# Block 2's mixing weights split into two parts during block 1's w_down and kept in DRAM; memory keys and values made earlier; the HGRN tail by head pair

## The chip, the cores and the metric

The kernel runs on one core of one Trainium2 chip. Its time is in device microseconds (us) from the start to the end of the program on that core. Engines are named as in the profile: PE is the matrix engine, PEld its weight loads, DVE the vector engine, ACT the activation engine, POOL GpSimd, SP the engine that issues most DMAs (its queue is SPq; ACTq is ACT's own).

## The reference, cut to what matters

Two transformer blocks run on 512 positions of width 1024 in float32. Block 1 mixes (convolution, block-sparse attention, memory attention, gates) and ends with a feed-forward net, FFN1: `w_up`, a convolution, gelu, `w_down`. Block 2, whose weights have the suffix `_2`, is what the change is about:

```python
h = rmsnorm_2(x, norm_mix[layer])
hq, hf, hi, hg, sq, sk, sv, iq, ik, iw, mq = split_in(h @ w_in[layer])
o_hg = hgrn2_mix(hq, hf, hi, hg, lb[layer], out_gain[layer])   # gated linear recurrence
o_sa = dsa_mix(sq, sk, sv, iq, ik, iw, ...)                    # top-256 keys by an index score
mem_n = rmsnorm_2(mem, norm_mem[layer])
o_mem = mem_mix(mq, mem_n, w_mem_kv[layer], ...)               # keys and values from mem alone
mixed = jnp.concatenate([o_hg, o_sa, o_mem], axis=-1)
x = x + mixed @ w_out[layer]
h = rmsnorm_2(x, norm_ffn[layer])
a, b = jnp.split(h @ w_ffn_in[layer], 2, axis=-1)
x = x + (silu(a) * b) @ w_ffn_out[layer]
```

The memory keys and values of block 2 need `mem_2` and `w_mem_kv_2` alone, and the split of a weight needs the weight alone; neither needs an activation.

## The kernel before, in words

**Products in three passes.** Every large product is made in the float32r type: each operand is split into a rounded part hi and a remainder lo, and PE does hi·hi, hi·lo and lo·hi (L175 to L177). Weights come in tiles of 128x1024 float32 (512 KB). `load` (L187) has SP bring a raw tile into one of three buffers of `rawp`; `split` has ACT make hi (a cast, L197) and then DVE make lo (a subtraction, L198). With `pr.on_pool` POOL does the subtraction; that is set for 16 tiles of block 2's mixing, w_mqsv to w_hq (the second half). hi and lo of a streamed tile take two of six buffers of `wp`, so three tiles are ready at most; "hold" and "res" tiles take buffers of the general pool `sp` (38 of 128x1024).

**Order of the work.** `Program` (L44 to L165) is a list of jobs, each with its weight tiles, written down in program order; each engine then runs its own instructions in that order. Before a job is recorded, tiles are loaded and split for it and up to two streamed tiles beyond (four "hold", six "res"). Background generators (index scores, top-k rounds, the recurrence, the attentions) advance by one step at each tick, a tick being one job or one part of a job, times their rate; `drain` runs a generator to its end. An engine stops where its next instruction has to wait, and what stands behind it in its order waits too.

**Stages of the time before.** QKV, convolution, attention and gates to 441 us; w_out to 487; `w_up` of FFN1 to 733; `w_down` to 855 (22 tiles of 24 matmuls; the last 4 are taken for each quarter of the positions in turn). Then block 2's mixing: w_hf and w_hq (first halves), w_ikw, w_iq, w_mqsv, w_mkv2, w_sqk, w_hf and w_hq (second halves), w_hi, w_hg. In the background run the gates, `hgrn_levels` (rate 0.5; DVE L1274 belongs to it), `idx` (index scores, then `top_keys`: rounds of MAX8, L1007, and MATCH_REPLACE8, L1008), the build of `memT2` (norm and transposes of the memory), the memory attention `mem2` and the selected attention `sa0` and `sa1`, one for each pair of heads. After w_hg `hgrn_levels` is drained, and `hgrn_tail` makes the output of the recurrence for all four heads of one quarter of the positions at a time: products L1399, square on ACT (L1401), sum on DVE, a power on POOL, scaling on DVE (L1406), the gate on POOL (L1408), transposes and L270/L275. w_out_2 follows in four steps of K (kp 0 to 3); kp 0 needs `mem2`, kp 1 needs `sa0` and `sa1`, kp 2 and 3 need the tail. L601 is the normalising of attention weights on ACT, L307 a transpose on PE, L618 attention weights times values. The second feed-forward net runs from 1200 us to the end.

## Time and profile before

| what | value |
|---|---|
| median of 3 runs | 1567.25 us (1565.92 to 1567.9) |
| the profiled execution's own time | 1568.02 us |
| its span, first to last instruction | 1566.2 us |
| mean granted clock of TensorE | 0.986 |
| chain that ended last, by engine | PE 82%, DVE 7%, ACT 4%, POOL 2%, issue 2%, DMA 2% |
| HBM read and written | 145.66 MB and 4.85 MB |

The span lies 1.8 us inside the execution's own time. Busy time of an engine is a share of the span; the chain says which engine's work ended last at each step. Times in us from the start of the span place a stage.

### The profile page before, as it was taken

To read this page: it belongs to the slowest core of one execution; us is meant where nothing else is said; L and a number is where in the kernel's file an instruction comes from. 1 tells how busy PE (TensorE), PEld (TensorE's weight loads), DVE (VectorE), ACT (ScalarE), POOL (GpSimd) and SP (SyncE) were. 2 spreads that over 40 slices of the span, in tenths; PEclk is the share of its full clock that TensorE was granted. 3 is DMA by queue.
4 is the path that set the end of the run, shared out by engine and by line. 5 is a ranking of instruction groups with operands and counts; after the bars stand their busy time and mean duration, and the time that the engine had idled before them with its cause. 6 is when DMAs were issued, how large, how long until landed. Compare 5 with 4: busy or idle time off the path is not lost.

```text
span 1566.2 us, 20399 instructions
## 1 busy us (share of the span) xinstructions
PE 1520.0 (97%) x8107; PEld 1261.1 (81%) x8107; DVE 789.3 (50%) x1200; ACT 597.5 (38%) x1043; POOL 238.3 (15%) x344
## 2 busy tenths in 40 slices
PE   8999999999999999999999999999789999999999
PEld 7887888888888888888888977677568888888887
DVE  5455453544446666665235488988545233333231
ACT  5454452433343433333234465455533222222120
POOL 1000000021102000000002197716220000000000
PEclk9999999999999999999999999999699999999999
DMA  5432243322252122223232331122222122222231
GB/s 187 99 106 73 83 128 108 121 81 81 96 164 78 68 95 99 102 96 107 95 137 92 115 119 70 68 75 82 68 81 81 68 94 95 94 102 100 94 121 54
DMA packets 46053, 151.83 MB, mean 97 GB/s; under 512 B 5476, under 2 KB 5988, under 8 KB 45958
## 3 DMA queue, kind: packets, MB, share of 16 engines
q1 hardware_dynamic: 41472, 142.62, 26.6%
q10 hardware_dynamic: 4486, 7.90, 1.8%
q8 instruction: 64, 1.05, 0.3%
q14 instruction: 31, 0.25, 0.0%
HBM read 145.66 MB, written 4.85 MB: 96 GB/s over the span
## 4 chain that ended last, share of the span: by engine, by line
PE 82%; DVE 7%; ACT 4%; POOL 2%; issue 2%; DMA 2%; ACTq 0%; SPq 0%; DVEq 0%; POOLq 0%
PE p L175 26%; PE p L176 26%; PE p L177 26%; PE p L307 2%; ACT s L592 1%; DVE s L1008 1%; DVE s L1274 1%; DVE m L1007 1%; PE p L618 1%; ACT s L601 1%; POOL m L228 1%; DVE wl L198 1%; DMA s<-mem 0%; POOL s L183 0%; DVE s L180 0%
## 5 line engine op out<-in xcount | busy, mean ns | idle before, releaser
L175 PE MATMUL p<-s,wh 128*128 128x512 f32 (+1 forms) x1192 | 463.6, 389 | 0.9 <-DVE t L1314 0.6
L176 PE MATMUL p<-s,wh 128*128 128x512 f32 (+1 forms) x1192 | 461.0, 387 | 0.0
L177 PE MATMUL p<-s,wl 128*128 128x512 f32 (+1 forms) x1192 | 460.7, 387 | 0.0
L198 DVE TENSOR_TENSOR wl<-r,wh 128x1024 fp32r<-128x1024 f32 x217 | 258.3, 1192 | 329.8 <-ACT wh L197 329.0
L197 ACT CAST wh<-r 128x1024 fp32r<-128x1024 f32 x233 | 232.9, 1002 | 230.8 <-PE p L176 219.2
L175 PEld LDWEIGHTS p<-s,wh 128*128 128x128 f32 x1192 | 224.0, 188 | 46.3 <-DVE t L1314 0.8
L177 PEld LDWEIGHTS p<-s,wl 128*128 128x128 f32 x1192 | 223.9, 188 | 45.5
L176 PEld LDWEIGHTS p<-s,wh 128*128 128x128 f32 x1192 | 224.0, 188 | 43.9
L175 PE MATMUL p<-wh,s 128*128 128x512 f32 x544 | 218.6, 402 | 4.1 <-ACT s L270 4.1
L177 PE MATMUL p<-wh,s 128*128 128x512 f32 x544 | 215.2, 396 | 1.0 <-DVE s L275 0.5
L176 PE MATMUL p<-wl,s 128*128 128x512 f32 x544 | 214.8, 395 | 0.0
L176 PE MATMUL p<-s,s 128*128 128x256 f32 (+1 forms) x408 | 132.2, 324 | 5.6 <-DVE s L180 5.6
L175 PE MATMUL p<-s,s 128*128 128x256 f32 (+1 forms) x408 | 133.2, 326 | 0.9 <-ACT s L268 0.8
L177 PE MATMUL p<-s,s 128*128 128x256 f32 (+1 forms) x408 | 131.6, 322 | 0.0
L183 POOL TENSOR_SCALAR s<-t 128x512 fp32r<-128x512 f32 (+1 forms) x64 | 34.7, 543 | 618.3 <-DVE t L1506 227.4
L175 PEld LDWEIGHTS p<-wh,s 128*128 128x128 f32 x544 | 104.0, 191 | 26.3 <-ACT s L270 4.5
L177 PEld LDWEIGHTS p<-wh,s 128*128 128x128 f32 x544 | 103.8, 191 | 24.2 <-DVE s L275 1.0
L176 PEld LDWEIGHTS p<-wl,s 128*128 128x128 f32 x544 | 104.1, 191 | 20.5
L176 PEld LDWEIGHTS p<-s,s 128*128 128x128 f32 x408 | 79.5, 195 | 11.9 <-DVE s L180 6.6
L175 PEld LDWEIGHTS p<-s,s 128*128 128x128 f32 x408 | 79.4, 195 | 7.1 <-ACT s L268 1.5
L177 PEld LDWEIGHTS p<-s,s 128*128 128x128 f32 x408 | 79.5, 195 | 5.3
L307 PE MATMUL p<-ident,s 128*128 128x128 f32 x400 | 59.7, 290 | 16.2 <-ACT s L601 4.8
(182 smaller groups left out, 1416.1 us busy)
## 6 DMA issues: line engine op xcount, KB each, us to landing
r<-w_up SPq DMA_DIRECT2D x44, 512.0 KB, 3.2
r<-w_ffn_in SPq DMA_DIRECT2D x44, 512.0 KB, 3.2
r<-w_in_gate SPq DMA_DIRECT2D x24, 512.0 KB, 3.2
r<-w_down SPq DMA_DIRECT2D x22, 512.0 KB, 3.2
r<-w_ffn_out SPq DMA_DIRECT2D x22, 512.0 KB, 3.2
r<-w_out SPq DMA_DIRECT2D x16, 512.0 KB, 3.2
r<-w_in_conv SPq DMA_DIRECT2D x12, 512.0 KB, 3.2
r<-w_in_qk SPq DMA_DIRECT2D x8, 512.0 KB, 4.6
```

What stands on the lines that cost most here:

```text
L175: mm(out, sh, mh, start=start, stop=False)
L176: mm(out, sh, ml, start=False, stop=False)
L177: mm(out, sl, mh, start=False, stop=stop)
L183: g_.tensor_scalar(out, x, s, 0.0, op0=ALU.mult, op1=ALU.add)
L197: a_.copy(hi[:, :n], raw)
L198: (g_ if on_pool else v_).tensor_tensor(out=lo[:, :n], in0=raw, in1=hi[:, :n].bitcast(F32), op=ALU.subtract)
L228: g_.tensor_tensor(out=rs, in0=ms, in1=negh[:, :n], op=ALU.pow)
L307: pe.transpose(ps[:m, n:n + P], s, ident)
L592: a_.activation(pv, pv, AF.Exp, scale=-1.0, bias=negm[s][:, i:i + 1], accum_out=sums[s][:, i:i + 1])
L601: a_.activation(pv, pv, AF.Copy, scale=rec[s][:, i:i + 1])
L618: mm(ps[64 * s:64 * s + 64, j * P:512], vh(s, j), p_view(PT, s, 3 - j), start=(j == 0), stop=(j == 3))
L1007: v_.max(m8, sc)
```

## The change

1. `pr.on_pool` goes; wherever a split is still made in place, DVE makes lo (now L204; the cast is L203, the raw load L189).
2. `Parts`: the 29 tiles of block 2's mixing weights (w_hf 4, w_hq 4, w_ikw 1, w_iq 4, w_mqsv 4, w_sqk 4, w_hi 4, w_hg 4) are split by a generator, "splits", at rate 0.5 during w_down. For each tile SP loads the raw tile into a buffer of `sp` (L216), ACT casts (L218), DVE subtracts (L219), and SP stores hi (L221) and lo (L222) to a DRAM tile `wd`. In the mixing, `split` loads both parts by two DMAs (L199, L200) into the buffers that the products read.
3. `memT2` is built from job 3 of w_up on, and the products with w_mkv2 and the finish of the keys (`fin_mkv2`) follow in w_up.
4. The mixing's products come in the order w_hf, w_hq (first halves), w_ikw, w_iq, w_mqsv, w_hf, w_hq (second halves), w_sqk, w_hi, w_hg. w_hg is now made in the transposed form, by chunks, and its weight is packed for that.
5. The tail is made per pair of heads j and half of the positions; `tail0` runs during w_hg. The gate's product is one DVE instruction with the gain (L1467) in place of a POOL one, then a cast on ACT (L1472) and a subtraction on DVE. `sa` runs the two pairs of the selected attention one after the other. w_out_2's kp 0 needs `mem2`, kp 1 `sa`, kp 2 and 3 `tail0` and `tail1`.

```diff
     def load(src):
+        if isinstance(src, Parts):
+            return src
         raw = rawp.tile([P, 1024], F32, tag="raw", name=nm("r"))[:, :src.shape[-1]]
         nc.sync.dma_start(raw, src)
         return raw
 
-    def split(raw, resident, on_pool):
-        n = raw.shape[-1]
+    def split(raw, resident):
         if resident:
             hi, lo = slot([P, 1024], F32R), slot([P, 1024], F32R)
         else:
             hi = wp.tile([P, 1024], F32R, tag="w", name=nm("wh"))
             lo = wp.tile([P, 1024], F32R, tag="w", name=nm("wl"))
+        if isinstance(raw, Parts):
+            nc.sync.dma_start(hi.bitcast(F32), raw.d[0])
+            nc.sync.dma_start(lo.bitcast(F32), raw.d[1])
+            return hi, lo
+        n = raw.shape[-1]
         a_.copy(hi[:, :n], raw)
-        (g_ if on_pool else v_).tensor_tensor(out=lo[:, :n], in0=raw, in1=hi[:, :n].bitcast(F32), op=ALU.subtract)
+        v_.tensor_tensor(out=lo[:, :n], in0=raw, in1=hi[:, :n].bitcast(F32), op=ALU.subtract)
         return hi, lo
+
+    class Parts:
+
+
+        def __init__(self, src):
+            self.src = src
+
+        def make(self):
+            raw, hi, lo = slot([P, 1024]), slot([P, 1024], F32R), slot([P, 1024], F32R)
+            self.d = drp.tile([2, P, 1024], F32, name=nm("wd"))
+            nc.sync.dma_start(raw, self.src)
+            yield
+            a_.copy(hi, raw)
+            v_.tensor_tensor(out=lo, in0=raw, in1=hi.bitcast(F32), op=ALU.subtract)
+            yield
+            nc.sync.dma_start(self.d[0], hi.bitcast(F32))
+            nc.sync.dma_start(self.d[1], lo.bitcast(F32))
 
     pr = Program(load, split)
...
     for j in range(2, NFF):
+        if j == 3:
+            pr.start("memT2", lambda: memT2.build())
+        if j == 8:
+            pr.drain("memT2")
+            gemm_N([io["w_mkv2"][i] for i in range(4)], lambda: memT2, lambda t, ps: use_mkv2(t, ps), nt=2)
+            pr.start("kv2", lambda: fin_mkv2())
         chunk(W[j], H, use_up_a(j))
         chunk(W[NFF + j], H, use_up_g(j))
-
+    pr.drain("kv2")
+
+    M = {n: [Parts(io[n][j]) for j in range(io[n].shape[0])]
+         for n in ("w_hf", "w_hq", "w_iq", "w_mqsv", "w_sqk", "w_hi", "w_hg")}
+    M["w_ikw"] = [Parts(io["w_ikw"])]
+    order = [M[n][c] for n in ("w_hf", "w_hq") for c in (0, 1)] + M["w_ikw"] + M["w_iq"] + M["w_mqsv"]
+    order += [M[n][c] for n in ("w_hf", "w_hq") for c in (2, 3)] + M["w_sqk"] + M["w_hi"] + M["w_hg"]
+
+    def splits():
+        made = [p.make() for p in order]
+        for n in range(len(made) + 2):
+            for p in made[max(0, n - 2):n + 1]:
+                next(p, None)
+            yield
+
+    pr.start("splits", splits, 0.5)
...
-    def hgrn_out(t):
+    def hgrn_out(j, tp):
+
         ps = bank()
-        for hd in range(4):
-            j, i2 = hd // 2, hd % 2
-            o = ps[:, hd * P:(hd + 1) * P]
-            ops = []
-            if t >= 2:
-                for s in range(2):
-                    ops.append((hg["o256"][j][:, i2, s, (t - 2) * P:(t - 1) * P], s))
-            if t % 2 == 1:
-                ops.append((hg["o128"][:, hd, t // 2, :], t - 1))
-            ops.append((hg["ATd"][j][:, i2, t, :], t))
-            for n, (l, s) in enumerate(ops):
-                mm(o, l, hi_[s // 2][:, s % 2, hd * P:(hd + 1) * P], start=(n == 0), stop=(n == len(ops) - 1))
+        for tt in range(2):
+            t = 2 * tp + tt
+            for i2 in range(2):
+                hd = 2 * j + i2
...
                          in1=rs[:, :, None].to_broadcast([P, 4, P]), op=ALU.mult)
-        g_.tensor_tensor(out=y, in0=y, in1=gS[t // 2][:, t % 2, :], op=ALU.mult)
         return y
...
+    def hgrn_outT(j, tp, y):
+
+        pt = transposes([y[:, (2 * t + k) * P:(2 * t + k + 1) * P] for k in range(2) for t in range(2)])
+        cols = slice(tp * 256, tp * 256 + 256)
+        z = tmp()
+        v_.scalar_tensor_tensor(z.rearrange("p (k t) -> p k t", k=2), pt.rearrange("p (k t) -> p k t", k=2),
+                                vcol(V_HG), gS[j][:, :, cols], op0=ALU.mult, op1=ALU.mult)
+        mixed.alloc(j)
+        hi, lo = mixed.h[j][:, :, cols], mixed.l[j][:, :, cols]
+        z = z.rearrange("p (k t) -> p k t", k=2)
+        a_.copy(hi, z)
+        sub_lo(lo, z, hi)
+
+    def hgrn_tail(j):
+        def g():
+            while ("done", 2 * j + 1) not in hg:
+                yield
+            y1 = hgrn_out(j, 1)
+            yield from wait(2)
+            y0 = hgrn_out(j, 0)
+            yield from wait(2)
+            while ("gate", j) not in hg:
+                yield
+            hgrn_outT(j, 1, y1)
+            yield from wait(2)
+            hgrn_outT(j, 0, y0)
+        return g
...
     def mixing():
-        next_head((late2, swap2), [io[n][c] for n in ("w_hf", "w_hq") for c in (0, 1)],
+        next_head((late2, swap2), [M[n][c] for n in ("w_hf", "w_hq") for c in (0, 1)],
                   [use_hf(0), use_hf(1), use_hq(0), use_hq(1)], park)
         pr.start("gates0", gates(0))
         pr.start("hgrn", hgrn_levels, 0.5)
-        chunk(io["w_ikw"], H, use_ikw)
+        chunk(M["w_ikw"][0], H, use_ikw)
         pr.start("idx", chain(sel0, index_weights, *(index_scores(c) for c in range(4)), top_keys(3),
                               top_keys(2), top_keys(1)), 0.6)
         for c in range(4):
-            chunk(io["w_iq"][c], H, use_iq(c))
-        pr.on_pool = True
-        pr.start("memT2", memT2.build)
-        gemm_N([io["w_mqsv"][j] for j in range(4)], H, use_mqsv)
+            chunk(M["w_iq"][c], H, use_iq(c))
+        gemm_N(M["w_mqsv"], H, use_mqsv)
         pr.start("finm", fin_mq)
-        pr.drain("memT2")
-        gemm_N([io["w_mkv2"][j] for j in range(4)], lambda: memT2, use_mkv2, nt=2)
-        pr.start("mem2", chain(fin_mkv2, mem2_pair(0), mem2_pair(1)), 0.5)
-        gemm_N([io["w_sqk"][j] for j in range(4)], H, use_sqk)
+        for c in (2, 3):
+            chunk(M["w_hf"][c], H, use_hf(c))
+        pr.drain("finm")
+        pr.start("mem2", chain(mem2_pair(0), mem2_pair(1)), 0.5)
+        for c in (2, 3):
+            chunk(M["w_hq"][c], H, use_hq(c))
+        pr.start("gates1", gates(1))
+        gemm_N(M["w_sqk"], H, use_sqk)
         pr.start("fin", fin_sqk)
-        for c in (2, 3):
-            chunk(io["w_hf"][c], H, use_hf(c))
-        for c in (2, 3):
-            chunk(io["w_hq"][c], H, use_hq(c))
-        pr.start("gates1", gates(1))
-        pr.rate("idx", 0.6)
-        pr.start("sa0", sa_pair(0), 0.5)
-        pr.start("sa1", sa_pair(1), 0.5)
-        pr.on_pool = False
-        gemm_N([io["w_hi"][j] for j in range(4)], H, use_hi)
-        gemm_N([io["w_hg"][j] for j in range(4)], H, use_hg)
-        pr.drain("hgrn")
-        pr.start("tail", hgrn_tail, 1.0)
+        gemm_N(M["w_hi"], H, use_hi)
+        pr.start("tail0", hgrn_tail(0))
+        pr.start("sa", chain(sa_pair(0), sa_pair(1)), 0.5)
+        pr.start("tail1", hgrn_tail(1))
+        for c in range(4):
+            chunk(M["w_hg"][c], H, use_hg(c))
...
-             need={0: ("mem2",), 1: ("sa0", "sa1"), 2: ("tail",)})
+             need={0: ("mem2",), 1: ("sa",), 2: ("tail0", "tail1")})
```

**SP in w_down.** Before, SP's order there held loads of w_down alone:

```order
L187 DMA r_6037<-w_down 128x1024
L187 DMA r_6067<-w_down 128x1024
L187 DMA r_6097<-w_down 128x1024
L187 DMA r_6127<-w_down 128x1024
L187 DMA r_6157<-w_down 128x1024
```

In the changed program one tile of w_down (r, from w_down) comes with two raw tiles of the mixing (s, from w_ikw and w_iq) and the stores of two others (wd):

```order
L189 DMA r_6157<-w_down 128x1024
L221 DMA wd_6130<-s_6128 128x1024
L222 DMA wd_6130<-s_6129 128x1024
L216 DMA s_6175<-w_ikw 128x1024
L221 DMA wd_6151<-s_6149 128x1024
L222 DMA wd_6151<-s_6150 128x1024
L216 DMA s_6196<-w_iq 128x1024
L189 DMA r_6205<-w_down 128x1024
```

Between two loads of w_down there now stand six more DMAs of 512 KB; a raw load stands behind the stores of an earlier tile.

**ACT in w_down.** Before, its casts there are those of w_down tiles (wh from r):

```order
L197 CAST wh_6033<-r_5947 128x1024
L197 CAST wh_6063<-r_5977 128x1024
L197 CAST wh_6093<-r_6007 128x1024
L197 CAST wh_6123<-r_6037 128x1024
L197 CAST wh_6153<-r_6067 128x1024
```

In the changed program two casts of mixing tiles (s from s) stand between two of w_down:

```order
L203 CAST wh_6201<-r_6063 128x1024
L218 CAST s_6197<-s_6196 128x1024
L218 CAST s_6224<-s_6223 128x1024
L203 CAST wh_6249<-r_6109 128x1024
L218 CAST s_6245<-s_6244 128x1024
L218 CAST s_6272<-s_6271 128x1024
L203 CAST wh_6297<-r_6157 128x1024
```

The cast of a w_down tile (wh_6297, whose raw load r_6157 is the first row of SP's piece above) now stands behind casts of mixing tiles whose raw loads SP issues later than r_6157: s_6271 is two loads of w_down later.

**PE at kp 1 of w_out_2.** Before, the products with the values (L618) of both pairs (p_9732, p_9745) stand side by side there, and each pair's scores long before:

```order
L1399 MATMUL p_9714<-s_8872,s_7002 128x128 x2
L1399 MATMUL p_9714<-s_8872,s_7003 128x128 x2
L618 MATMUL p_9732<-s_9516,s_7571 64x512 x2
L618 MATMUL p_9732<-s_9523,s_7571 64x384 x2
L618 MATMUL p_9732<-s_9528,s_7571 64x256 x2
L618 MATMUL p_9732<-s_9523,s_7571 64x128 x2
L618 MATMUL p_9745<-s_9535,s_7571 64x512 x2
L618 MATMUL p_9745<-s_9542,s_7571 64x384 x2
L618 MATMUL p_9745<-s_9547,s_7571 64x256 x2
L618 MATMUL p_9745<-s_9542,s_7571 64x128 x2
L307 MATMUL p_9756<-ident,s_9664 128x128 x4
L175 MATMUL p_9563<-wh_9129,s_9741 128x512
```

In the changed program pair 1's scores (L581, L582) stand behind pair 0's products with the values (L641):

```order
L641 MATMUL p_9864<-s_9834,s_7912 64x512 x2
L641 MATMUL p_9864<-s_9841,s_7912 64x384 x2
L641 MATMUL p_9864<-s_9846,s_7912 64x256 x2
L641 MATMUL p_9864<-s_9841,s_7912 64x128 x2
L581 MATMUL p_9883<-s_8840,s_8837 128x512
L582 MATMUL p_9883<-s_8842,s_8837 128x512
L581 MATMUL p_9886<-s_8840,s_8838 128x512
L582 MATMUL p_9886<-s_8842,s_8838 128x512
```

Pair 1's other twelve score products, its transposes and its own eight products with the values follow with nothing else between, and only then the first pass of kp 1. All of pair 1, from scores to values, now stands behind pair 0.

## Rows read from the trace of the kernel before

**Rows 1.** The page's head, whole program: span, then busy time, share and instructions by engine
```profile
span 1566.2 us, 20399 instructions
...
PE 1520.0 (97%) x8107; PEld 1261.1 (81%) x8107; DVE 789.3 (50%) x1200; ACT 597.5 (38%) x1043; POOL 238.3 (15%) x344
```

**Rows 2.** Windows by stage: bounds, length, busy by engine, granted clock, DMA share, GB/s
```profile
487.00:733.00 246.00, 243.78 (x1166) 206.24 (x1167) 151.11 (x189) 92.90 (x125) 16.11 (x28) 0.99 0.25 88
733.00:855.00 122.00, 122.00 (x548) 101.13 (x546) 45.01 (x50) 36.35 (x59) 7.08 (x13) 1.00 0.34 117
855.00:911.00 56.00, 54.17 (x342) 48.84 (x341) 30.95 (x43) 29.29 (x47) 16.55 (x26) 1.00 0.25 90
911.00:1069.00 158.00, 145.69 (x1064) 111.86 (x1062) 133.80 (x251) 87.52 (x186) 99.85 (x124) 0.98 0.24 82
...
1097.00:1162.00 65.00, 48.24 (x555) 39.20 (x553) 37.14 (x97) 32.77 (x72) 20.95 (x36) 0.79 0.22 72
```

**Rows 3.** Lines in 733:855: count, busy, mean ns, idle before and its releaser
```profile
L177 PE MATMUL p<-wh,s 128*128 128x512 f32 x144 | 56.0, 389 | 0.0
...
L198 DVE TENSOR_TENSOR wl<-r,wh 128x1024 fp32r<-128x1024 f32 x17 | 20.8, 1224 | 53.9 <-ACT wh L197 53.9
L197 ACT CAST wh<-r 128x1024 fp32r<-128x1024 f32 x16 | 16.8, 1053 | 59.6 <-PE p L176 59.6
```

**Rows 4.** Waits of SP's DMA queue in 733:855: total us, times, longest
```profile
SPq L187 <- DVE wl L198: 80.9, 17, 7.2
```

**Rows 5.** DMA issues, whole program: queue, count, size, median us to landing
```profile
r<-w_down SPq DMA_DIRECT2D x22, 512.0 KB, 3.2
...
xdram<-s ACTq DMA_DIRECT2D x4, 512.0 KB, 2.6
```

**Rows 6.** Windows in which the DMA engines are full or nearly so
```profile
8.00:12.00 4.00, 2.61 (x13) 2.21 (x12) 2.19 (x5) 3.08 (x8) 0.86 (x2) 1.00 1.02 382
10.00:12.00 2.00, 1.39 (x7) 1.39 (x8) 2.00 (x5) 1.09 (x2) 0.00 (x0) 1.00 1.03 410
874.00:880.00 6.00, 6.00 (x53) 6.00 (x52) 0.20 (x1) 1.19 (x2) 0.00 (x0) 1.00 0.88 350
```

**Rows 7.** Lines by shape in 911:1069, the middle of block 2's mixing
```profile
L198 POOL TENSOR_TENSOR wl<-r,wh 128x1024 fp32r<-128x1024 f32 x15 | 36.7, 2448 | 14.6 <-ACT wh L197 11.3 <-issue 3.0 <-DVE s L1274 0.3
...
L197 ACT CAST wh<-r 128x1024 fp32r<-128x1024 f32 x20 | 21.0, 1049 | 0.0
L1274 DVE TENSOR_TENSOR s<-s,s 128x256 f32<-128x256 f32 x18 | 18.9, 1050 | 1.4 <-ACT s L1271 1.4
...
L198 DVE TENSOR_TENSOR wl<-r,wh 128x1024 fp32r<-128x1024 f32 x6 | 8.4, 1403 | 7.4 <-ACT wh L197 7.4
```

**Rows 8.** Waits of PE in 911:1069
```profile
PE p L307 <- DVE s L180: 4.4, 1, 4.4
```

**Rows 9.** Lines by shape in 1097:1162, the end of the mixing
```profile
L1274 DVE TENSOR_TENSOR s<-s,s 128x256 f32<-128x256 f32 x9 | 4.9, 547 | 1.3 <-ACT s L1271 1.3
...
L1007 DVE MAX8 m<-s 128x8 f32<-128x256 f32 x9 | 3.8, 417 | 0.0
L1008 DVE MATCH_REPLACE8 s<-m,s 128x256 f32<-128x256 f32 x9 | 3.7, 409 | 0.0
```

**Rows 10.** Timeline of ACT in the same stretch: start, us, instruction
```profile
1118.16 7.33 ACT L601 ACTIVATE s<-s,m 128x512 f32<-128x512 f32 x16
```

**Rows 11.** Timeline of PE there: start, us, instruction, idle before it
```profile
1120.12 2.39 PE L307 MATMUL p<-ident,s 128*128 128x128 f32 x10 [2.26 <-ACT s L601]
...
1145.57 4.53 PE L618 MATMUL p<-s,s 128*64 128x512 f32 x32
...
1161.96 0.50 PE L175 MATMUL p<-wh,s 128*128 128x512 f32 x1 [4.10 <-ACT s L270]
```

**Rows 12.** Two windows around a pause of PE: columns as in Rows 2
```profile
939.00:944.00 5.00, 0.59 (x6) 0.39 (x5) 4.76 (x8) 1.14 (x2) 1.32 (x3) 1.00 0.18 73
944.00:948.00 4.00, 4.00 (x14) 3.20 (x13) 2.21 (x6) 2.19 (x4) 1.97 (x1) 0.57 0.00 0
```

More of the change, by code (lines that the diff above doesn't have):

```diff
@@ L49, in __init__ @@
         self.loaded, self.got = [], []
-        self.jobs, self.bg, self.held, self.on_pool = [], {}, 0, False
+        self.jobs, self.bg, self.held = [], {}, 0
     def job(self, fn, tiles=(), kind="w", step=True, prefetch=True):
-        self.jobs.append((fn, [(t, kind, self.on_pool) for t in tiles], step, prefetch))
+        self.jobs.append((fn, [(t, kind) for t in tiles], step, prefetch))
     def ctl(self, fn, prefetch=True):
@@ L91, in prepare @@
         n = len(self.got)
-        kind, on_pool = self.flat[n][1:]
-        self.got.append(self.split(self.loaded[n], kind != "w", on_pool))
+        kind = self.flat[n][1]
+        self.got.append(self.split(self.loaded[n], kind != "w"))
         self.loaded[n] = None
@@ L1318, in hgrn_products @@
                     pool_scale(ATd[r, i2, :, r], hg["acc"][r])
+                hg["done", hd] = True
     def hgrn_levels():
@@ L1369, in use_hi, with use_hg, f @@
         a_.copy(hi_[t // 2][:, t % 2, :], ps)
-    def use_hg(t, ps):
-        if t % 2 == 0:
-            gS[t // 2] = slot([P, 2, 512])
-        silu2(gS[t // 2][:, t % 2, :], ps)
+    def use_hg(c):
+        def f(ps):
+            if c % 2 == 0:
+                gS[c // 2] = slot([P, 2, 512])
+            silu2(gS[c // 2][:, c % 2, :], ps)
+            if c % 2:
+                hg["gate", c // 2] = True
+        return f
     def sa_pair(c):
@@ L1384, in sa_pair @@
         return g
[L1386 removed]
+    def hgrn_out(j, tp):
         ps = bank()
[L1388 to L1399 removed]
+        for tt in range(2):
+            t = 2 * tp + tt
+            for i2 in range(2):
+                hd = 2 * j + i2
+                o = ps[:, (2 * tt + i2) * P:(2 * tt + i2 + 1) * P]
+                ops = []
+                if t >= 2:
+                    for s in range(2):
+                        ops.append((hg["o256"][j][:, i2, s, (t - 2) * P:(t - 1) * P], s))
+                if t % 2 == 1:
+                    ops.append((hg["o128"][:, hd, t // 2, :], t - 1))
+                ops.append((hg["ATd"][j][:, i2, t, :], t))
+                for n, (l, s) in enumerate(ops):
+                    mm(o, l, hi_[s // 2][:, s % 2, hd * P:(hd + 1) * P], start=(n == 0), stop=(n == len(ops) - 1))
         sqr = tmp()
@@ L1609, in _layout @@
     io["w_hi"] = _pack_n(w[:, 1024:1536])
-    io["w_hg"] = _pack_n(w[:, 1536:2048])
+    io["w_hg"] = _pack_t(w[:, 1536:2048])
     io["w_sqk"] = _pack_n(w[:, 2048:2560])
```

14 lines of the change are left out of this document (removed).

## The prediction, before the run

> **What bounds the kernel now.** I read the page's head first: PE is busy for 1520.0 of 1566.2 us [rows 1], so a change can win only the 46 us in which PE idles and the time it spends at a low clock, and it can lose wherever it makes PE wait. The windows by stage say where that margin lies [rows 2]: none in w_down (122.00 of 122), 2 us in w_up, 1.8 in 855:911, 12.3 in 911:1069, and 16.8 at a granted clock of 0.79 in the last stretch of the mixing. The change adds its work to the one stage of these that has no margin, so the next view is what supplies PE there. A w_down tile is 24 matmuls, 8 at each of the three lines; their records overlap (144 busy for 56.0 us at one line [rows 3]), so I take a tile's cost from the window: 122.00 us less 0.5 for the end of w_up and 1.7 for the transposes of the next head, over 22 tiles, is 5.44 us a tile. ACT and DVE pay 1.05 and 1.22 us a tile [rows 3], and SP's queue waits 80.9 us there for DVE to free a raw buffer [rows 4]: the DMA engines are mostly idle (share 0.34 [rows 2]). So before, PE alone sets the pace of w_down.
>
> **What the DMA engines can carry.** With all 16 engines full, the program's start shows 382 and 410 GB/s at shares of 1.02 and 1.03 [rows 6]. At 400 GB/s a 512 KB tile (524,288 bytes) takes 1.31 us of all engines, 1.28 at 410 and 1.37 at 382. One alone lands 3.2 us after issue, a store 2.6 [rows 5]. A store is no cheaper: in 874:880, where the four xdram stores run beside weight loads, the two together move 350 GB/s at a share of 0.88, which is 398 at full share [rows 6].
>
> A page of the Trainium skill speaks against the change here: "DMA: Bandwidth & Descriptors", Specifications, puts the HBM limit of one core at about 358 GB/s. By that, a tile would take 1.46 us and the first term below would be about +60 instead of +45; the trace shows 382 to 410 [rows 6], so the rows decide.
>
> **The terms.**
>
> 1. *w_down.* Two mixing tiles are split per w_down job, as SP's order shows: 2 raw loads, 4 stores and 1 w_down load, seven DMAs of 1.31 us, 9.2 us against 5.44 us of PE. PE then waits in every job. It cannot run ahead either: ACT's order puts the casts of two mixing tiles ahead of each w_down cast, and those tiles' raw loads come later in SP's queue than the w_down tile itself. So w_down tile 17 (counted from 0) is cast only after the 29th mixing tile. From the first split load to that one SP issues 99 DMAs (29 raw loads, 54 stores, 14 w_down tiles, 2 gains): 99 x 1.31 = 130 us. Behind it come its landing (3.2 - 1.3 = 1.9) and two casts and one subtraction (2 x 1.05 + 1.22 = 3.3): 135 us. Then five jobs are left, 5 x 5.44 = 27.2, and 1.7 of transposes. After pauses PE starts slowly: behind a pause of over 4 us the clock was granted at 0.57 over the next 4 us [rows 12], that is mostly the lower of its levels, 1.2 of 2.4 GHz; restarting so costs 4 x 0.43 = 1.7 us once, and nothing while DMA sets the pace (5.44 + 1.7 is under 9.2). Sum 165.6 against 121.5: I take **+45**. Ends: at 410 GB/s 126.7 instead of 130 gives +41, at 382 136 gives +51. DVE and ACT hold it: 45.0 + 29 x 1.22 = 80 and 36.4 + 29 x 1.05 = 67 us, of over 165 [rows 2, 3]. Nothing is hidden on SP's queue: of what it is moved past, the first eight DMAs of the mixing's parts stand behind the last stores, 8 x 1.31 = 10.5 us, covered by the last five jobs.
>
> 2. *The mixing, 855 to 1097.* Out go, in 911:1069 alone, 15 POOL subtractions (36.7 us), 20 casts (21.0) and 6 DVE subtractions (8.4) [rows 7], and the memory's norm, transposes and key finish, one step of which PE waits 4.4 us for [rows 8]. DVE also gets quicker where POOL is quiet: L1274 takes 1050 ns beside POOL's subtractions and 547 at the end [rows 7, 9]. In come two loads a tile, 2.6 us per 5.44, hidden by PE; if that cover went, a tile would cost their landing, 3 us. What can be won is PE's idle time of 12.3 us and 0.02 x 158 = 3.2 of clock, with 1.8 in 855:911 at most 17 [rows 2]. DVE was busy for 133.8 of 158 us there and had waits on both sides; I keep a third of the idle time, for waits that the new order makes (gates, sqk and `sa` come later): **-11**, ends 0 and -17.
>
> 3. *The end of the mixing.* From the end of w_hg at 1097.3 to kp 2's first pass at 1161.96 [rows 11] were 64.7 us. Now: eleven rounds of MAX8 and MATCH_REPLACE8 (0.83 us a pair [rows 9], 0.86 with their gap) are still to do, 9.5 us, and between them DVE's part of `tail1` and the last of the recurrence, some 7.5: 17. Pair 0's last scores and exponentials 3.5, its normalising half of 7.33 = 3.7 [rows 10], transposes 2 x 2.4, its products half of 4.53 = 2.3 [rows 11]: about 31. Pair 1, alone behind it: eight score sums and exponentials about 8 (estimated from these), normalising 3.7, transposes partly beside it 3, products 2.3, hi and lo 1.2: 18, so 49. kp 1 with 5.4 to 9 (half clock), and kp 2 starts at 54 to 58, 7 to 11 us early. Against that stand POOL's powers and two more waits on ticks in `tail1`, which this sum treats as covered by DVE. I keep half of the smaller figure, **-4**, ends -10 and +12, the latter if pair 1's 18 us come on top of the old path but for the 3.7 and 2.3 that it paid there.
>
> 4. *Memory keys and values in w_up.* The 48 matmuls and the transposes only move, PE's work in all is the same. w_up has DVE busy 151 and ACT 93 of 246 us [rows 2], DMA at 0.25: **0**, ends 0 and +3 (a drain at job 8 that has to wait).
>
> The gate's product on DVE instead of POOL adds four instructions of about 0.7 us, counted in term 3.
>
> Sum against the profiled execution's own 1568.0 us: 1568 + 45 - 11 - 4 + 0 = **1598 us**. Its 1568.0 stands 0.8 above the median of 1567.25, less than the 0.2% (3 us) that a measurement of this kernel can tell from no change.
>
> **Rivals.**
>
> (a) *Loads and stores pass each other.* If a DMA engine's reading and writing ran side by side, so that stores to DRAM went beside loads, a job would need the larger of 3 loads (3.9 us) and 4 stores (5.2 us), under 5.44, and w_down would stay at PE's pace, with about 2 us of start. It decides as soon as a DMA costs under 0.78 us (5.44 / 7). The time: 1568 + 2 - 11 - 4 = 1555, faster than before. For it: no window before has stores and loads in such a mix. Against it: 874:880 has both, and their sum stays on the same 400 GB/s per full share [rows 6]. "DMA: Bandwidth & Descriptors" of the Trainium skill, in "Two DMAs through the same engine are not ordered", says that an engine's read and write sides are separate queues; by that rule alone it could go this way, and no run here shows it. Chance 0.12.
>
> (b) *The chain of one tile, not the bandwidth.* A raw load waits in SP's order behind the two stores of a tile before it (2.6), lands (3.2), and two casts of others and its own, and two subtractions follow (2 x 1.05 + 2 x 1.22 = 4.5) before its own stores. If nothing else fills the queue meanwhile, that is 10.3 us for each two tiles, 14.5 x 10.3 = 149 in place of 130: +64, and 1568 + 64 - 11 - 4 = 1617. For it: three tiles only are in flight, and the waits of SP's queue for DVE are already long [rows 4]. Against: other tiles' stores and the w_down load stand ready during the casts. Chance 0.18.
>
> (c) *The mixing and its end win nothing*, because a new wait takes the place of the old: 1568 + 45 + 0 + 10 = 1623. Chance 0.08.
>
> (d) *The two sides cancel*: stores cheaper than loads, so that term 1 is only some +15, with terms 2 and 3 as forecast: within 0.2% of 1568. Chance 0.03.
>
> My forecast with its bounds keeps 0.59: -17 and -10 with +41 give 1582, 0 and +12 with +51 give 1631, and (b), (c) lie inside. Below, the case of (a) is left out (0.12), and beyond the top (b) with (c) together, 1568 + 64 + 10 = 1642. The range is 1580 to 1634. Chances: faster 0.13, (a) and the lower edge; same 0.03; slower 0.84.
>
> **What would show it.** Right: w_down's stage 160 to 172 us long with a DMA share near 1.0 and about 400 GB/s over it, PE waiting at L175 for ACT's cast or DVE's lo, the granted clock low there, and raw loads landing in well over 3.2 us; the mixing from its head to w_hg's end about 231 us with hardly an L203 or L204 in it; pair 1 alone on PE ahead of kp 1. Term 1 is wrong if w_down's DMA share stays under 0.9 (then (b)) or its stage near 125 (then (a)); term 2 if PE's idle time in the mixing is still 12 us; term 3 if the time from the end of w_hg to kp 2 is over 70.

## The result, and where the time went

The changed kernel takes 1655.0 us (median of 4 runs, 1654.2 to 1656.8), against 1566.7 for the kernel before, measured beside it: a ratio of 1.0565, with a 95% interval of 1.0546 to 1.0583. It was forecast slower, at 1598, but the time lies 21 us above the range. The page's head and HBM row of the changed kernel answer to [rows 1]:

```profile
span 1652.6 us, 20600 instructions
...
PE 1551.3 (94%) x8107; PEld 1278.4 (77%) x8107; DVE 793.0 (48%) x1216; ACT 597.6 (36%) x1039; POOL 185.2 (11%) x324
...
HBM read 176.07 MB, written 35.26 MB: 128 GB/s over the span
```

The program wrote 30 MB more to DRAM and read 30 MB more: 29 tiles in two parts each, as the change says. PE is busy for 31 us longer with the same 8107 records, since more of them ran at the lower clock: in w_down alone its busy time went from 122.00 [rows 2] to 158.75 us, at a mean granted clock of 0.83 in place of 1.00. The span is 86.4 us longer. The windows by stage (columns as in [rows 2]) are w_up with w_mkv2, w_down, the mixing to the end of w_hi, and from w_hg to the second feed-forward net:

```profile
485.00:749.00 264.00, 259.19 (x1238) 218.76 (x1239) 164.15 (x209) 104.28 (x150) 21.86 (x36) 0.99 0.28 96
749.00:960.00 211.00, 158.75 (x545) 120.49 (x545) 74.63 (x75) 59.86 (x81) 5.04 (x11) 0.83 0.81 301
960.00:1152.00 192.00, 185.16 (x1487) 151.23 (x1486) 125.62 (x262) 90.46 (x198) 78.10 (x142) 0.98 0.36 127
1152.00:1287.00 135.00, 109.13 (x796) 88.14 (x797) 79.19 (x186) 52.11 (x116) 19.15 (x39) 0.89 0.26 90
```

The stage that had no idle time before, 122.00 of 122 us [rows 2], now is 211 us long, with PE busy for 159 of them at a clock of 0.83, and the DMA engines not full either: 0.81 of their time, 301 GB/s. What PE waited for over the whole program is read from its waits (total us, times, longest); the two for split tiles, 40.6 and 11.9, lie nearly all in w_down and make up the 52 us that PE idles there:

```profile
PE p L175 <- ACT wh L203: 40.6, 14, 6.2
...
PE p L176 <- DVE wl L204: 11.9, 15, 1.0
```

To compare stages exactly I paired PE's records with PE's order of instructions, so a stage goes from its first pass to the next stage's first pass. Here and for the experiments (us; profiled executions):

| kernel | w_up (with w_mkv2 where it is there) | w_down | mixing and w_out_2 | median of the runs |
|---|---|---|---|---|
| before | 246.4 | 121.5 | 345.3 | 1567 |
| changed | 264.3 | 211.0 | 326.1 | 1655.0 |
| late_cast | 263.4 | 164.0 | 325.6 | 1613.4 |
| no_stores | 264.8 | 167.2 | 326.0 | 1612.9 |
| no_parts | 264.8 | 121.5 | 338.4 | 1578.4 |
| spread | 271.1 | 122.2 | 327.2 | 1574.3 |
| parts_old | 244.9 | 121.5 | 327.9 | 1547.5 |
| parts_keys | 270.7 | 122.3 | 329.5 | 1575.9 |
| parts_order | 272.1 | 122.2 | 318.8 | 1566.3 |
| parts_rates | 246.4 | 121.5 | 322.9 | 1543.9 |
| sa_two | 270.6 | 122.2 | 327.2 | 1571.2 |
| sa_last | 272.2 | 122.2 | 331.7 | 1578.2 |
| sa_last_two | 285.7 | 124.7 | 326.7 | 1593.1 |

The stages are those of the one execution that was profiled. For late_cast that is the fastest of four, 1606.1 us, 7 us under the median; for sa_two it is the slowest of twelve, 1574.9.

So w_down is 89.5 us longer, w_up another 17.9 (13.5 of it work that moved there), and the mixing with w_out_2 gives back 19.2 (though the same 13.5 us of PE's work left it); the start of the program took 1.8 us less. The sum is the 86.4 of the span.

**One turn of w_down.** SP's DMA issues in the changed kernel, one turn of two mixing tiles and one w_down tile (start, us of issue, what; a turn runs from one L189 to the next):

```profile
809.74 0.33 SPq L189 DMA_DIRECT2D r<-w_down  x1
810.12 0.42 SPq L221 DMA_DIRECT2D wd<-s  x1
810.60 0.42 SPq L222 DMA_DIRECT2D wd<-s  x1
811.07 1.33 SPq L216 DMA_DIRECT2D s<-w_mqsv  x1
812.50 1.20 SPq L221 DMA_DIRECT2D wd<-s  x1
813.80 0.45 SPq L222 DMA_DIRECT2D wd<-s  x1
814.30 0.48 SPq L216 DMA_DIRECT2D s<-w_mqsv  x1
821.14 0.33 SPq L189 DMA_DIRECT2D r<-w_down  x1
```

All seven DMAs are issued within 5 us, and then SP's queue stands for 6.4 us before the next w_down load (L189). Its waits in the stage name what it waits for, as in [rows 4]:

```profile
SPq L189 <- DVE wl L204: 101.8, 17, 6.9
```

L189 needs one of three raw buffers, and that is freed by DVE's subtraction for an earlier w_down tile. ACT and DVE in the same turn:

```profile
806.27 1.04 ACT L218 CAST s<-s 128x1024 fp32r<-128x1024 f32 x1 [6.57 <-DMA s<-w_iq]
807.23 1.04 ACT L203 CAST wh<-r 128x1024 fp32r<-128x1024 f32 x1
810.02 1.05 ACT L218 CAST s<-s 128x1024 fp32r<-128x1024 f32 x1 [1.76 <-DMA s<-w_mqsv]
817.67 1.04 ACT L218 CAST s<-s 128x1024 fp32r<-128x1024 f32 x1 [6.60 <-DMA s<-w_mqsv]
818.62 1.04 ACT L203 CAST wh<-r 128x1024 fp32r<-128x1024 f32 x1
```

```profile
808.49 1.22 DVE L204 TENSOR_TENSOR wl<-r,wh 128x1024 fp32r<-128x1024 f32 x1
...
819.89 1.22 DVE L204 TENSOR_TENSOR wl<-r,wh 128x1024 fp32r<-128x1024 f32 x1
```

The w_down cast (L203, 818.62) stands on ACT right behind the cast of a mixing tile (L218, 817.67), and that one had waited 6.60 us for its raw load, which SP issued at 811.07, behind the L189 of 809.74. This is a loop: L189, the raw load behind it, its landing, the cast, the w_down cast, the subtraction, the next L189. 809.74 to 821.14 is 11.4 us. The DMA engines meanwhile run full and then stand mostly empty (2 us windows of that turn):

```profile
809.00:811.00 2.00, 1.41 (x4) 1.04 (x4) 0.71 (x1) 0.98 (x1) 0.00 (x0) 0.50 0.31 59
...
815.00:817.00 2.00, 2.00 (x10) 1.65 (x9) 0.00 (x0) 0.00 (x0) 0.00 (x0) 1.00 1.02 414
817.00:819.00 2.00, 0.69 (x4) 0.23 (x2) 0.25 (x1) 1.33 (x2) 0.00 (x0) 1.00 1.02 416
```

At full share they move 414 to 416 GB/s with loads and stores mixed, so seven DMAs need 8.8 us (an estimate from these two rows); the other 2.6 us of the turn stay unused.

### The profile page after: what moved, and what is told of

It is laid out like the page before. It is cut to its first block, busy times and chain, and to the rows that moved or that the text cites. A ratio compares the mean times of both kernels' runs of the same rounds, so it can differ in the third digit from the quotient of the medians.

```text
span 1652.6 us, 20600 instructions
## 1 busy us (share of the span) xinstructions
PE 1551.3 (94%) x8107; PEld 1278.4 (77%) x8107; DVE 793.0 (48%) x1216; ACT 597.6 (36%) x1039; POOL 185.2 (11%) x324
## 4 chain that ended last, share of the span: by engine, by line
PE 76%; DVE 7%; DMA 7%; ACT 4%; issue 2%; SPq 2%; POOL 1%; ACTq 0%; DVEq 0%; POOLq 0%
PE p L175 24%; PE p L176 24%; PE p L177 23%; PE p L330 3%; DVE wl L204 1%; DMA s<-w_iq 1%; ACT s L615 1%; DVE s L1052 1%; PE p L641 1%; DMA s<-w_hq 1%; DMA s<-w_mqsv 1%; DMA s<-w_sqk 1%; DMA s<-w_hi 1%; DMA s<-w_hg 1%; DVE m L1051 1%
## 5 line engine op out<-in xcount | busy, mean ns | idle before, releaser
L175 PE MATMUL p<-s,wh 128*128 128x512 f32 (+1 forms) x1224 | 477.4, 390 | 0.0
L176 PE MATMUL p<-s,wh 128*128 128x512 f32 (+1 forms) x1224 | 473.7, 387 | 0.0
L177 PE MATMUL p<-s,wl 128*128 128x512 f32 (+1 forms) x1224 | 473.5, 387 | 0.0
L204 DVE TENSOR_TENSOR wl<-r,wh 128x1024 fp32r<-128x1024 f32 x208 | 246.5, 1187 | 269.9 <-ACT wh L203 267.4
L203 ACT CAST wh<-r 128x1024 fp32r<-128x1024 f32 x208 | 206.6, 995 | 172.5 <-PE p L176 158.7
L177 PEld LDWEIGHTS p<-s,wl 128*128 128x128 f32 x1224 | 230.1, 188 | 47.1
L175 PEld LDWEIGHTS p<-s,wh 128*128 128x128 f32 x1224 | 230.3, 188 | 45.7 <-issue 0.7
L176 PEld LDWEIGHTS p<-s,wh 128*128 128x128 f32 x1224 | 230.4, 188 | 44.9
L175 PE MATMUL p<-wh,s 128*128 128x512 f32 x512 | 215.8, 421 | 40.6 <-ACT wh L203 40.6
L176 PE MATMUL p<-wl,s 128*128 128x512 f32 x512 | 214.2, 418 | 11.9 <-DVE wl L204 11.9
L177 PE MATMUL p<-wh,s 128*128 128x512 f32 x512 | 210.8, 412 | 0.0
L219 DVE TENSOR_TENSOR s<-s,s 128x1024 fp32r<-128x1024 f32 x29 | 35.5, 1224 | 112.1 <-ACT s L218 112.1
L176 PEld LDWEIGHTS p<-s,s 128*128 128x128 f32 x408 | 79.0, 194 | 12.2 <-DVE s L180 6.9
L330 PE MATMUL p<-ident,s 128*128 128x128 f32 x400 | 62.3, 304 | 27.7 <-ACT s L624 14.1
L175 PEld LDWEIGHTS p<-s,s 128*128 128x128 f32 x408 | 78.8, 193 | 6.7 <-ACT s L291 1.0
```

The source lines that it names most:

```text
L175: mm(out, sh, mh, start=start, stop=False)
L176: mm(out, sh, ml, start=False, stop=False)
L177: mm(out, sl, mh, start=False, stop=stop)
L203: a_.copy(hi[:, :n], raw)
L204: v_.tensor_tensor(out=lo[:, :n], in0=raw, in1=hi[:, :n].bitcast(F32), op=ALU.subtract)
L219: v_.tensor_tensor(out=lo, in0=raw, in1=hi.bitcast(F32), op=ALU.subtract)
```

## The experiments

**late_cast: open the loop.** Each raw load gets a step of lead before its cast:

```diff
             nc.sync.dma_start(raw, self.src)
             yield
+            yield
             a_.copy(hi, raw)
...
-        for n in range(len(made) + 2):
-            for p in made[max(0, n - 2):n + 1]:
+        for n in range(len(made) + 3):
+            for p in made[max(0, n - 3):n + 1]:
```

> The changed kernel, but each mixing tile's cast and subtraction come one step of the generator later after its raw load (four tiles in flight instead of three). Loop theory: in w_down SP's queue stands at the w_down load (L189), because the raw buffer is freed by the w_down tile's subtraction, whose cast stands on ACT behind a mixing cast that waits for a raw load behind that very L189; a turn is 11.4 us for seven DMAs that need 8.8 us at 418 GB/s. With the raw load a step earlier the loop no longer closes on a fresh load, and the DMA engines set the turn, 8.8 to 9.2 us: 14 turns save 31 to 36 us, so about 1620 us (1612 to 1628), with w_down at a DMA share near 1.0. Rival, bandwidth: loads and stores mixed simply cost 11.4/7 = 1.6 us each, then nothing changes: 1650 to 1658.

Measured: 1613.4 us (1606.1 to 1613.9), ratio 1.0286 (1.0266 to 1.0305), 42 us under the changed kernel, with not a byte less to move. Windows of w_down and of its middle, and ACT's w_down casts there:

```profile
749.00:913.00 164.00, 136.92 (x545) 106.56 (x543) 74.11 (x74) 60.94 (x84) 5.73 (x13) 0.92 0.97 382
770.00:900.00 130.00, 103.01 (x388) 78.56 (x387) 55.45 (x51) 46.29 (x56) 1.75 (x4) 0.89 1.00 397
```

```profile
806.94 1.04 ACT L203 CAST wh<-r 128x1024 fp32r<-128x1024 f32 x1
...
815.68 1.04 ACT L203 CAST wh<-r 128x1024 fp32r<-128x1024 f32 x1
...
824.42 1.05 ACT L203 CAST wh<-r 128x1024 fp32r<-128x1024 f32 x1
```

The turn is 8.74 us and the DMA engines are full: 397 GB/s at a share of 1.00 over 130 us. The loop theory holds and the bandwidth rival falls. With the loop open, w_down takes 164.0 us in this execution, where the prediction's first term had 165.6; the other three took 7 us longer, and no trace says in which stage, so the match is that close for this one alone. The Trainium skill ("DMA: Bandwidth & Descriptors", Specifications) gives about 358 GB/s of HBM for a core, a stack's 716 divided by its two cores. The trace does not keep to that share: one core ran, and 397 GB/s held over 130 us of loads and stores. Not tried were two other edits that might open the same loop: a fourth raw buffer, and the w_down cast ahead of the mixing casts in ACT's order.

**no_stores: take the bytes away and leave the loop.** Only the first tile's parts are stored, and all tiles are loaded from them:

```diff
+            first = Parts.d0 is None
+            if first:
+                Parts.d0 = drp.tile([2, P, 1024], F32, name=nm("wd"))
+            self.d = Parts.d0
...
-            nc.sync.dma_start(self.d[0], hi.bitcast(F32))
-            nc.sync.dma_start(self.d[1], lo.bitcast(F32))
+            if first:
+                nc.sync.dma_start(self.d[0], hi.bitcast(F32))
+                nc.sync.dma_start(self.d[1], lo.bitcast(F32))
```

> The changed kernel, but only the first mixing tile's parts are stored, and every tile is loaded from those: all products of block 2's mixing use the parts of w_hf's first tile. 56 of 58 stores go. Loop theory: the turn stays a loop, but with one w_down load and one raw load in it instead of four DMAs: 0.8 of issue, 2 x 1.25, 1.4 of landing, two casts 2.0, a subtraction 1.2 = about 7.5 to 7.9 us, still over PE's 5.44: w_down about 155 to 160 us, the time about 1600 (1592 to 1610), at a DMA share of only 0.5 in w_down. Rival, bandwidth: three DMAs need under 5.44 us, so w_down goes back to 122 to 126 and the time to 1566 to 1572.

Measured: 1612.9 us (1610.9 to 1613.4), ratio 1.0291 (1.0277 to 1.0305). The middle of w_down, SP's issues and ACT's casts in one turn:

```profile
770.00:900.00 130.00, 104.64 (x373) 78.59 (x372) 55.02 (x49) 46.67 (x53) 0.00 (x0) 0.88 0.54 201
```

```profile
810.39 0.33 SPq L189 DMA_DIRECT2D r<-w_down  x1
810.77 0.66 SPq L220 DMA_DIRECT2D s<-w_mqsv  x1
...
819.15 0.33 SPq L189 DMA_DIRECT2D r<-w_down  x1
```

```profile
815.67 1.05 ACT L222 CAST s<-s 128x1024 fp32r<-128x1024 f32 x1 [5.81 <-DMA s<-w_mqsv]
816.62 1.04 ACT L203 CAST wh<-r 128x1024 fp32r<-128x1024 f32 x1
...
824.88 1.04 ACT L203 CAST wh<-r 128x1024 fp32r<-128x1024 f32 x1
```

Nearly half of the DMA time is free (share 0.54), and still PE does not get back to its 5.44 us a tile: a turn takes 8.3 (cast to cast) to 8.8 us (L189 to L189). So the loop alone, without any lack of bandwidth, costs w_down 46 us; the bandwidth rival (1566 to 1572) is out. The time lies 3 us above the range of the loop theory (1592 to 1610): the turn is some 0.7 us longer than I had put it, as the cast of the raw load starts 4.9 us after its issue (810.77 to 815.67). Two other loads are issued within a microsecond of it; that they take their share of the engines is read from these times, not tested.

**no_parts: the rest of the change alone.** The mixing weights are split in place, the generator is not started:

```diff
-    M = {n: [Parts(io[n][j]) for j in range(io[n].shape[0])]
+    M = {n: [io[n][j] for j in range(io[n].shape[0])]
...
-    pr.start("splits", splits, 0.5)
```

> The changed kernel without Parts: the mixing weights are loaded raw and split by ACT and DVE in the mixing, all else (order, keys in w_up, tail by pair) as changed. w_down goes back to 121.5 us, which takes 89.5 off 1655: 1565. Theory A: the mixing's gain of about 6 us in the changed kernel comes from the order and the removal of the key build, and DVE has room for 29 subtractions of 1.22 us (35 us): 1563 to 1570. Theory B: the gain came from the splits' leaving the mixing; with all 29 on DVE (16 were on POOL before) PE waits for DVE there: 1575 to 1585.

Measured: 1578.4 us (1576.6 to 1579.6), ratio 1.0071 (1.0058 to 1.0083): theory B. w_down is back at 121.5, and the mixing is 12.3 us longer than with parked parts (338.4 against 326.1). The window of w_sqk in this kernel, and then in the changed one:

```profile
993.00:1032.00 39.00, 32.59 (x316) 24.77 (x303) 35.18 (x69) 19.62 (x36) 21.89 (x43) 0.96 0.24 75
```

```profile
1080.00:1110.00 30.00, 30.00 (x296) 23.39 (x297) 26.61 (x59) 15.38 (x30) 14.75 (x37) 1.00 0.42 150
```

PE's longest wait there in no_parts:

```profile
PE p L581 <- DVE t L1357: 3.7, 1, 3.7
```

With its splits DVE has 8.6 us more to do in this stage, which is 9 us longer, and PE idles for 6.4 us of it, where it idles for nothing in the changed kernel. DVE's share is 0.9 in both; what differs is the amount of its work. The 12.3 us price parking against a mixing with all 29 subtractions on DVE; 16 of them were on POOL before. This kernel, with order, early keys, tail and those 16 on DVE, loses 11 us against the kernel before.

**spread: the same bytes over 370 us.** The splits start at job 2 of w_up at rate 0.15 (lo overwrites raw, so a tile needs two buffers):

```diff
+        if j == 2:
+            pr.start("splits", splits, 0.15)
...
-            raw, hi, lo = slot([P, 1024]), slot([P, 1024], F32R), slot([P, 1024], F32R)
+            raw, hi = slot([P, 1024]), slot([P, 1024], F32R)
+            lo = raw.bitcast(F32R)
...
-    pr.start("splits", splits, 0.5)
```

> The changed kernel with the 29 splits spread from job 2 of w_up to job 15 of w_down (rate 0.15 instead of 0.5, lo written over the raw tile, so two buffers a tile). About one tile in 1.7 jobs: 3 x 1.25 us of DMA in 9 us beside 1.7 loads. Loop theory: a raw load is then out long before its cast, so no loop closes and w_up and w_down stay at PE's pace: 1655 - 89.5 + up to 5 = 1563 to 1571. Rival: every split tile holds up ACT's queue for its landing, some 2 us each for 29 tiles: 1600 to 1630.

Measured: 1574.3 us (1574.1 to 1575.6), ratio 1.0049 (1.0035 to 1.0063), 3 us over what the loop theory gave. w_down is at 122.2: 81 of the changed kernel's 88 us were the rush. w_up is 6.8 us longer than the changed kernel's. PE's longest wait in it falls at the jobs of w_mkv2:

```profile
PE p L176 <- DVE wl L204: 2.9, 1, 2.9
```

The granted clock is 0.85 over the 10 us behind it, so some 4 to 5 us are lost there (an estimate from the two). Those jobs are half as long and bring the same number of ticks, so the splits come twice as fast; that this is the cause is argued, and sa_last_two below, which moved the splits behind these jobs, did not get shorter.

**parts_old: parking alone.** The kernel before, with `Parts` and the spread generator, and nothing else of the change (its own order, tail and key build).

> The kernel before, with its own order, tail and key build, and only the parking of the 29 tiles added, spread over w_up and w_down (rate 0.15 from job 2 of w_up, lo over the raw tile). It says what parked parts are worth by themselves. Theory A (the splits' leaving the mixing is the gain of term 2): 11 of the 28 us that the mixing before loses up to w_hi come back, less 2 to 5 for the spread: 1558 to 1563. Theory B (the gain came from the order and the early keys): 1566 to 1572.

Measured: **1547.5 us** (1546.2 to 1548.2), ratio 0.9877 (0.9864 to 0.9890), 11 us better than theory A. Its windows of w_up, w_down, the mixing to the end of w_hi, and from w_hg to the second feed-forward net:

```profile
484.00:729.00 245.00, 242.83 (x1170) 205.13 (x1169) 174.05 (x211) 114.98 (x148) 16.17 (x28) 1.00 0.64 224
729.00:850.00 121.00, 121.00 (x543) 100.38 (x542) 48.61 (x54) 39.64 (x62) 5.87 (x13) 1.00 0.68 251
850.00:1048.00 198.00, 194.16 (x1406) 159.67 (x1405) 144.37 (x290) 97.18 (x211) 86.01 (x138) 0.99 0.41 142
1048.00:1178.00 130.00, 111.59 (x945) 90.26 (x944) 72.50 (x171) 57.73 (x127) 33.14 (x57) 0.89 0.27 93
```

w_up and w_down carry the splits at a DMA share of about 0.65 without a loss. PE idles 3.8 of 198 us in the mixing, where it idled 14.1 of 214 before (1.8 and 12.3 [rows 2]), and its busy time is 5.7 us shorter with the same products; POOL is busy for 86 us instead of 116. From w_hg on nothing changes (130 us, 131 before). Whether it is DVE, POOL or ACT whose relief counts was not tested apart.

**parts_keys and parts_order: the other parts, one at a time on top.** First the early keys (`memT2` from job 3 of w_up, w_mkv2 at job 8; `mem2` started behind w_sqk), then also the order of the products, the gates and `mem2` as in the change; the tail and the selected attention stay as before.

> The kernel before with the parking spread (1547.5 us), and the memory keys and values made in w_up as the change does; the memory attention starts behind w_sqk. In the changed kernel w_up lost 4.3 us more than before beside the 13.5 that moved. If that is the price of the early keys, and the mixing's wait of 2.5 us for the memory's transposes goes with it: 1547 to 1553. Rival: the half-length jobs of w_mkv2 collide with the splits in w_up as in the spread kernel (6.6 more): 1553 to 1558.

> The same with the changed order of the products as well (w_hf and w_hq's second halves ahead of w_sqk, the memory attention and the gates where the change has them), the tail and the selected attention as before. In the spread kernel w_hi lost 10 us and the end of the mixing 6 us more than in the kernel before with parking. Theory: w_hi's loss belongs to the order, since the memory attention falls into w_hi: 10 us over the one with early keys alone, the rest up to 1574 is the tail's. Rival: all 20 belong to the new tail, and this one stays within 3 us of the one with early keys.

Measured: parts_keys 1575.9 us (1574.7 to 1577.5), far above both of my figures; parts_order 1566.3 (1563.6 to 1568.4). The table of stages shows why. With early keys w_up is 25.8 us longer than in parts_old: 13.5 for the work that moved, 4.4 more that the changed kernel pays there too (17.9 in all), and 8 that come only where early keys and splits are both in w_up. And the mixing, from which those 13.5 us of PE work were taken, is not shorter: 329.5 against 327.9. Its windows in parts_keys, to be held against the last two rows of parts_old:

```profile
879.00:1070.00 191.00, 182.86 (x1321) 150.02 (x1322) 123.65 (x259) 85.60 (x187) 68.50 (x126) 0.97 0.37 127
1070.00:1208.00 138.00, 113.66 (x955) 92.80 (x954) 77.05 (x188) 57.15 (x127) 33.54 (x59) 0.86 0.25 88
```

PE idles for 32.5 us in the two instead of 22.3, and the granted clock is lower in both: what was taken away has become waiting. (`mem2` also starts later in parts_keys, so the early keys do not stand quite alone there.) The order then wins 9.5 us (318.8), so my theory on the order was wrong, and from there to spread (1574.3) the new tail with its chained pairs and the transposed w_hg costs 8: that part of the rival holds.

So the steps from before to the changed kernel, by medians: parking, spread, -20; early keys +28; order -9.5; tail +8; the rush of the splits in w_down +81.

**sa_two, sa_last, sa_last_two: the end of the mixing.** On spread: the pairs side by side as before; or w_out_2 with the selected attention as its last K step; or both, with the splits from job 9 of w_up at rate 0.18.

```diff
-        pr.start("sa", chain(sa_pair(0), sa_pair(1)), 0.5)
+        pr.start("sa0", sa_pair(0), 0.5)
+        pr.start("sa1", sa_pair(1), 0.5)
...
-    korder = [6, 7, 4, 5, 0, 1, 2, 3]
+    korder = [6, 7, 0, 1, 2, 3, 4, 5]
...
-             need={0: ("mem2",), 1: ("sa",), 2: ("tail0", "tail1")})
+             need={0: ("mem2",), 1: ("tail0",), 2: ("tail1",), 3: ("sa",)})
```

> The spread kernel, but the two pairs of the selected attention run side by side again (two generators at rate 0.5) instead of one behind the other. If pair 1 alone behind pair 0 is what the end of the mixing pays, kp 1 starts about 8 us earlier (selection done, then 16 scalings of 0.46, transposes and products of both pairs in one go, instead of 15.9 us of pair 1 behind pair 0's products): 1563 to 1568 against 1574. Rival: the rounds of the selection set the end and pair 1 costs nothing: 1572 to 1576.

> The spread kernel, but w_out_2 takes its K steps in the order memory, tail of pair 0, tail of pair 1, selected attention (the weight packed to fit), so that the selected attention is needed 2 steps later. If it is the chain of the selected attention that PE waits for (36 us lost in w_out_2), two steps of 10.9 us slide under it: 1574 - 22, with less half clock perhaps - 26: 1547 to 1554. Rival: the chain's instructions are recorded by ticks and stand behind the passes anyway, so that it starts later too: 1562 to 1574.

> Both of the above, and the splits spread from job 9 of w_up (rate 0.18), behind the products with w_mkv2, where the spread kernel lost 5 us in a half-length job. If the prices add: 1574 - 22 - 4 (of the 8, as steps slide under) - 6 = 1542 (1538 to 1550). Rival: as soon as the chain is hidden, pairs side by side bring nothing: 1546 to 1552.

Measured: sa_two 1571.2 (1565.0 to 1574.9), not clear: its median is 3 us under spread's and between the two theories, and its profiled execution, the slowest, has the same mixing of 327.2 us as spread. sa_last 1578.2 (1576.4 to 1580.1), sa_last_two 1593.1 (1589.8 to 1594.9): both worse, against the theory. One of sa_last's waits of PE behind w_hg, DVE's last round of the selection there, and then that round in spread:

```profile
PE p L1453 <- POOL s L183: 7.4, 1, 7.4
```

```profile
1149.24 0.43 DVE L1053 MAX8 m<-s 128x8 f32<-128x256 f32 x1
```

```profile
1138.39 0.43 DVE L1053 MAX8 m<-s 128x8 f32<-128x256 f32 x1
```

The last round comes 43.6 us after w_out_2's first pass (1105.6) instead of 32.7 (1105.7 in spread): the chain starts later too, as the rival said. That the later drain puts the generators' steps later in DVE's order is argued from the program. PE now waits 7.4 us for the tail's power on POOL, 1.9 in spread. The hoped-for 22 us were too many in any case: a step of w_out_2 is 5.5 us in the changed kernel at the full clock (kp 1 from 1246.58 to 1252.15), so two are 11. In sa_last_two it is w_up that went from 271 to 286 us, and PE waits there for the split of w_up's own tiles:

```profile
PE p L177 <- DVE wl L204: 7.3, 5, 3.2
PE p L175 <- ACT wh L203: 5.4, 3, 2.7
```

Why a later start at nearly the same rate brings these waits was not tried.

**parts_rates: the best version.** parts_old, with the room on DVE used:

```diff
-        pr.rate("idx", 0.6)
+        pr.rate("idx", 0.8)
+        pr.rate("hgrn", 0.7)
```

> The kernel before with the parking spread (1547.5 us), with the index scores' and top-k rounds' generator at rate 0.8 instead of 0.6 and the recurrence's at 0.7 instead of 0.5 from w_hi on. In w_hi and w_hg DVE has a third of its time free once the splits are parked, so 6 rounds of 0.86 us and 6 steps of the recurrence leave the stretch behind w_hg: 1537 to 1543. Rival: DVE's rows in w_hi and w_hg then hold up PE as much as they save: 1545 to 1550.

Measured: **1543.9 us** (1543.3 to 1544.9), ratio 0.9855 (0.9841 to 0.9868) of the kernel before: faster than both kernels, and between the two theories. The table has the gain over parts_old in the mixing (322.9 against 327.9); the 1.5 us by which w_up differs are chance, as the edit does not touch it. Which of the two rates wins was not tried apart.

## Why the prediction was wrong, point by point

- **Term 1, w_down, +45; measured +89.5.** This step failed. It took a turn for "seven DMAs of 1.31 us, 9.2 us against 5.44 us of PE", that is, the bandwidth for the only thing that paces w_down. The bandwidth itself was right (late_cast: 8.74 / 7 = 1.25 us a DMA in the middle, 1.29 over fourteen turns). What was missing is the loop through the raw buffer, which makes a turn 11.4 us. Fourteen turns, from the L189 at 763.78 to that at 928.95, take 165 us, 11.8 each; in late_cast, from 756.43 to 883.24, they take 127, 9.1 each. That is 38 of the 47 us between the two profiled executions; the rest lies at the stage's ends, 6.5 of it ahead of these turns. By the medians of all runs opening the loop is worth 42 us. The row was there: SP's queue waited 80.9 us for DVE's subtraction [rows 4]. I read that as "the DMA engines are mostly idle" and not as "SP's queue is held here, and everything put behind it in its order is held too". I had even named the casts that wait for later loads, and took from it only where the stage ends. The prediction's own sign points the same way: a DMA share under 0.9 in w_down was to speak for rival (b), and it was 0.81.
- **Slower, as forecast.** That was no luck: with the loop open (late_cast) the kernel is still 46 us slower than before, and w_down 42.5 us longer in the profiled execution, as term 1 had it. With the loop and without the stores (no_stores) it is 46 us slower too. In the middle of the stage each alone gives a turn of 8.3 to 8.8 us, about 3 over PE's 5.44, and both together 11.4, 6 over it.
- **Rival (b), a chain instead of the bandwidth, 1617.** The right kind, the wrong loop: it went through the stores and gave 10.3 us a turn; the loop goes through L189 and gave 11.4. no_stores shows that the loop closes without the stores: a turn still takes 8.3 to 8.8. In the changed kernel they lengthen it: two stand between L189 and the raw load (1.33 us instead of 0.38), and the cast starts 6.6 us after that load's issue instead of 4.9.
- **Rival (a), stores beside loads for nothing.** Fell: in late_cast three loads and four stores fill a turn of 8.74 us at full share. Had they passed each other, the DMAs of a turn would have needed the four stores' 5.2 us. The Trainium skill ("DMA: Bandwidth & Descriptors", "Two DMAs through the same engine are not ordered") says that read and write sides are separate queues, and says nothing of their rate; the trace has no gain from it.
- **Term 2, the mixing, -11.** Right in its cause: parking takes 12.3 us off the mixing with the new order (no_parts against changed, where no_parts has all subtractions on DVE) and 17.4 with the old one (parts_old against before), at the upper end of 17. Its sign does not contradict: up to the end of w_hi PE idles for 6.8 us instead of 14.1. The other sign, 231 us from the mixing's head to w_hg's end, was put wrongly: it did not take off the 13.5 us that term 4 moves out of that stretch. Measured are 226 (960 to 1186), against 242 before.
- **Term 3, the end, -4 with ends -10 and +12.** The step from parts_order to spread puts the new tail at +8 for the whole mixing. By the term's own bounds, from the end of w_hg to kp 2's first pass, it is +2 in the changed kernel: w_out_2's first pass is at 1185.93 there, kp 1 starts at 1246.58, 61 us later where the sum had 49, and kp 2 some 66 us later, against 64.7 before. Both figures are inside the ends, of the other sign. kp 2's first pass:

```profile
1252.15 0.39 PE L175 MATMUL p<-wh,s 128*128 128x512 f32 x1
```

- **Term 4, early keys, 0 to +3.** Wrong in kind. w_up grew by 17.9 us, of which 13.5 moved: 48 matmuls of 0.227 and 24 transposes of 0.109, all in a stage that PE bounds. I set those off against the mixing. parts_keys shows that taking it away there shortens nothing, and that PE idles instead. The likely reason is that in the mixing PE's work was cover for DVE's rounds and the recurrence, whose generators advance by ticks of PE's jobs; this is argued, not tested. In my sum "the work only moves" was worth 0; it costs what moves.
- Terms 2 to 4 together: forecast -15; measured -19.2 + 17.9 = -1.3. With +89.5 and the 1.8 us that the program's start took less, that is the 86.4 of the span, against +30 forecast.
